# Layer 0's attention scores: the whole-array products of two tiles first, then the small products of both

## The chip, the cores and the metric

The kernel runs on one core of a Trainium2 chip. The core has five engines with queues of their own: TensorE (PE in the profile; PEld is its loading of weights), VectorE (DVE), ScalarE (ACT), GpSimd (POOL) and SyncE (SP), which here issues nearly all DMAs. Each engine works through its queue in order; engines wait for each other by semaphores. The metric is the device time of one execution in microseconds, less is better.

## What is computed

The reference is a decoder trunk of two layers over 256 tokens of width 1024, in float32. Layer 0 mixes tokens by dilated causal attention in three groups, layer 1 by gated linear attention; both are followed by a gated convolution FFN.

```python
A_CONFIGS = ((128, 1), (512, 4), (2048, 16))     # window, dilation
...
qkv = (h @ w_in).reshape(B, S, A_GROUPS, 3, A_HEADS, A_HEAD_DIM)
for g, (window, dilation) in enumerate(A_CONFIGS):
    o, lse = dilated_branch(q_g * scale, k_g, v_g, rel_bias_g, window, dilation)
...
wts = softmax(lses over the groups)
o = sum(wts * outs)
```

In a branch, token t attends to tokens t − j·dilation inside the window: s = q·k + bias, p = exp(s − max), o = p·v / sum. The softmax over the three groups' normalizers makes the whole one softmax over the keys of all three groups, which is how the kernel does it.

## The kernel before

**Split products.** Most weights are float32 and are multiplied in three passes: `split` loads 2048 columns into a raw buffer (L159, four buffers, shared with the chunks of `ada_chunk`, L133), ACT copies them to a rounded high part (L165, `whi`), DVE subtracts to get the low part (L168, `wlo`), and `mm3` multiplies high·high, low·high and high·low (L174 to L176).

**Units of layer 0.** The 16 heads are taken as eight units of two heads (`for u in range(NPAIR)`, L455). The weights of units 0 and 1 come with the first load. Each unit from 2 on projects q and k for three groups (tile `pqk`, three loads of 1 MB from `in_wqk`), and each from 1 on projects v (tile `pv`, two loads from `in_wv`). `evacuate` takes q and k out of PSUM: group 0's q becomes a high part on ACT (L434) and a low part on DVE (L435), one of each for each head; its k a high part on ACT (L439) and a low part on DVE (L440); groups 1 and 2 stay plain (L429, L430). `by_group` takes v out (L447 to L450). Between these, `next_ada` computes chunks of the conditioning products on DVE (L138).

**The attention of a unit** (`attend`, L356). The 256 tokens are in order of their residue modulo 4. There are four score tiles, one for each residue r, in PSUM banks of the tag `s`, of which there are three. A tile's rows are 64 queries of each of two heads. `shared` makes the columns of group 0: three products of the whole 128x128 array (L367), about 256 columns each. `dilated` adds 64 columns for group 1 and 64 for group 2: for each group and head one product of 64x64 (L374), which the profile records as two instructions. So a tile has four small products, eight records.

Tiles are handled in two pairs (h = 0, 1). DVE adds the bias and takes the maximum (L385, once a tile), negates it (L391, once a pair), ACT exponentiates (L394, once a tile), DVE takes the reciprocal (L395, once a pair) and scales the probabilities (L400 and L401, once a tile). PE transposes them (L405, three a tile), DVE and ACT in turn copy the result out (L406), and PE multiplies by v (L410, L414, tile `po`), which is again taken apart (L419 on ACT, L420 on DVE).

**What sets the order.** The program is written unit by unit, but the order on each engine is not the written one: a scheduler works on an estimated timeline when the program is built, and puts each instruction into its engine's queue. `behind(i)` adds one constraint, that what is made inside it is placed after instruction i in that order. In the built program the scores of a unit stand among the products of v and the next unit's projections. Once built, the order is fixed.

Of the kernel before, what the change touches and what calls it, by code (L numbers as in the profile page):

```python
# [57 lines left out]
def trunk(ctx: ExitStack, tc: tile.TileContext, I, out):  # L58
# [13 lines left out]
    def bank(name="ps", tag=None):  # L72
        tag = tag or next(cycle)
        return psum.tile([P, 512], F32, tag=tag, name=name, bufs={"p": 2, "s": 3, "t": 3}[tag])

    mm = nc.tensor.matmul
# [106 lines left out]
    def rstd_of(squares, n=D, tag=None):  # L183
        ps = bank("ms", tag)
        for i, sq in enumerate(squares):
            a = mm(ps[:, :T], ones_d, sq, start=(i == 0), stop=(i == len(squares) - 1))
        ln = tmp.tile([P, T], F32, tag="ln", name="ln", bufs=2)
        nc.scalar.activation(ln, ps[:, :T], AF.Ln, bias=eps[:, 0:1], scale=D / n)
        r = tmp.tile([P, T], F32, tag="rstd", name="rstd", bufs=2)
        norm_ops[:] = a, nc.scalar.activation(r, ln, AF.Exp, scale=-0.5)  # L190
        return r
# [29 lines left out]
    def by_residue(ap):  # L221

        return ap.rearrange("p (i r) -> p r i", r=4)

    def in_order(ap):

        return ap.rearrange("p (r i) -> p i r", r=4)

    def grouped(ap):
        return ap.rearrange("p (r i) -> p r i", r=4)  # L230

    def as_tokens(ap):
        return ap.rearrange("p (i r) -> p i r", r=4)
# [4 lines left out]
    @contextmanager  # L238
    def behind(*those):

        with ExitStack() as st:
            for i in those:
                st.enter_context(tc.issue_after(i.ins))
            yield
# [20 lines left out]
    def all_normed(l, sub):  # L265
        r = rstd_of([sums[0], sums[1], sums[2]])
        with behind(norm_ops[0]):
            keep_warm(6)
        return [normed(l, sub, r, kt) for kt in range(KT)]
# [45 lines left out]
    r = rstd_of([sq[:, 0, :], sq[:, 4, :]])  # L315
# [11 lines left out]
    w0, h = [], []  # L327
# [28 lines left out]
    def attend(u, q, k, v, bias):  # L356


        m = tmp.tile([P, 16], F32, tag="m", name="m")
        prob = [att.tile([P, KEYS + 3], F32, tag="prob", name="prob", bufs=6) for _ in range(4)]  # L360
        pt = att.tile([P, 4, KEYS], F32, tag="pt", name="pt")
        heads = [slice(E * hh, E * hh + E) for hh in range(2)]

        def shared(s, r):
            n = T + r + r % 2
            for i, (a, b) in enumerate(((0, 0), (1, 0), (0, 1))):
                mm(s[:, 0:n], q[0][a][:, r].rearrange("p a b -> p (a b)"), k[0][b][:, 0:n], start=(i == 0), stop=(i == 2))  # L367

        def dilated(s, r):
            own = slice(CH * r, CH * r + CH)  # L370
            for g in (1, 2):
                at = T + r + CH * (g - 1)
                for e in heads:
                    mm(s[e, at : at + CH], q[g][e, own], k[g][e, own], start=True, stop=True)  # L374

        for h in range(2):
            s = [bank("s", "s") for _ in range(2)]
            shared(s[0], 2 * h)
            dilated(s[0], 2 * h)
            shared(s[1], 2 * h + 1)  # L380
            dilated(s[1], 2 * h + 1)
            for i in range(2):
                r = 2 * h + i
                back = bass.AP(bias.tensor, bias.offset + KEYS - 1 + r, [bias.ap[0], [-1, KEYS + r]])
                nc.vector.tensor_tensor_reduce(  # L385
                    prob[r][:, 0 : KEYS + r], s[i][:, 0 : KEYS + r], back,
                    op0=ALU.add, op1=ALU.max, scale=1.0, scalar=-3e38, accum_out=m[:, r : r + 1],
                )
        for h in range(2):
            rs = slice(2 * h, 2 * h + 2)  # L390
            nc.vector.tensor_scalar(m[:, 4:8][:, rs], m[:, 0:4][:, rs], -1.0, None, op0=ALU.mult)  # L391
            for r in (2 * h, 2 * h + 1):
                c = prob[r][:, 0 : KEYS + r]
                nc.scalar.activation(c, c, AF.Exp, bias=m[:, 4 + r : 5 + r], accum_out=m[:, 8 + r : 9 + r])  # L394
            nc.vector.reciprocal(m[:, 12:16][:, rs], m[:, 8:12][:, rs])  # L395
            for r in (2 * h, 2 * h + 1):

                f = m[:, 12 + r : 13 + r]
                pn = att.tile([P, KEYS], F32, tag="pn", name="pn", bufs=3)
                nc.vector.tensor_scalar(grouped(pn[:, 0:T]), by_residue(prob[r][:, 0:T]), f, None, op0=ALU.mult)  # L400
                nc.vector.tensor_scalar(pn[:, T:KEYS], prob[r][:, T + r : KEYS + r], f, None, op0=ALU.mult)  # L401
                t = bank("t", "t")
                for j in range(3):
                    c = slice(P * j, P * j + P)
                    nc.tensor.transpose(t[:, c], pn[:, c], ident)  # L405
                (nc.vector.tensor_copy if r % 2 else nc.scalar.copy)(pt[:, r, :], t[:, 0:KEYS])  # L406
        po = bank("po", "t")
        for n in range(2):
            for hh, e in enumerate(heads):
                mm(grouped(po[e, :T]), v[n][:, e], pt[:, :, P * n + E * hh : P * n + E * hh + E], start=(n == 0), stop=False)  # L410
        for r in range(4):
            for hh, e in enumerate(heads):
                at = P * (r % 2) + P + E * hh
                mm(po[e, CH * r : CH * r + CH], v[r // 2][:, at : at + E],  # L414
                   pt[:, r, T + E * hh : T + E * hh + E], start=False, stop=(r == 3))
        hi = att.tile([P, T], F32R, tag=f"ohi{u}", name="ohi", bufs=1)
        lo = att.tile([P, T], F32R, tag=f"olo{u}", name="olo", bufs=1)
        src, hv, lv = in_order(po[:, :T]), as_tokens(hi), as_tokens(lo)
        nc.scalar.copy(hv, src)  # L419
        nc.vector.tensor_tensor(lv, src, hv.bitcast(F32), op=ALU.subtract)  # L420
        o_hi.append(hi)
        o_lo.append(lo)
# [32 lines left out]
    for u in range(NPAIR):  # L455
        with tc.issue_after(last_load[0].ins):
            bias = load_bias(u)
        q = [q_pair[u % 2]]
        k = [[att.tile([P, T + 4], F32R, tag=f"k0{i}", name="k") for i in range(2)]]
# [6 lines left out]
        if u == 0:  # L466
# [5 lines left out]
            for kt in range(KT):  # L472
                s, e = kt == 0, kt == KT - 1
# [11 lines left out]
        else:  # L485
            for g in range(NG):
# [3 lines left out]
                for kt in range(KT):  # L490
                    s, e = kt == 0, kt == KT - 1
# [15 lines left out]
        for n in range(2):  # L507
            by_group(v[n], pv[n], n)
        attend(u, q, k, v, bias)
        if u == 1:  # L510
            for n in range(2):
# [93 lines left out]
    h = all_normed(1, 0)  # L605
# [163 lines left out]
    for n in range(4):  # L769
        r = r_g[n // 2][:, 2 * (n % 2) : 2 * (n % 2) + 2, :]  # L770
        with behind(*norm_ops):
            silu = nc.scalar.activation(r, r, AF.Silu)
        for et in range(2):
            i = 2 * n + et
# [18 lines left out]
    def turned(tiles):  # L793
        for kt in tiles:
            for t, own in enumerate(halves):
                i = nc.tensor.transpose(y_ps[t][kt // 4][:, P * (kt % 4) : P * (kt % 4) + P], x[kt][:, own], ident)
        return i

    def mean_square(parts):
        for part in parts:  # L800
            for t, own in enumerate(halves):
                i = mm(ps[:, 2 * t : 2 * t + 2], sums[part][:, own], ones_d[:, 0:2], start=(part == t == 0), stop=(part == 2 and t == 1))
        return i

    with behind(last_pd[0]):
        last = mean_square(range(2))
    with behind(last):
        last = turned(range(2))
    with behind(last):
        last = mean_square([2])  # L810
# [4 lines left out]
    r = tmp.tile([P, 4], F32, tag="m", name="rstd")  # L815
# [111 lines left out]
```

## Time and profile before

| | us |
|---|---|
| median of 3 runs | 803.75 |
| lowest, highest | 802.86, 808.61 |
| the profiled execution | 802.44 |
| its span, first to last instruction | 800.7 |

The granted clock of TensorE is 0.995 of full speed over the span. The attention of layer 0 takes PE from 67 us (the first score product) to 285 us (the last product with v); the first FFN follows at 301 us. By tile, the whole-array score products are 96 instructions (L367) and the small ones 256 records (L374), the first at 66.7 and 67.4 us, the last at 273.2 and 273.6 us.

In the rows of a timeline, the first number is the start in us from the span's start, the second the length in us, then engine, line, operation, out<-in, shape and how many were merged; in square brackets stands how long the engine was idle before it and what ended that. Matmuls are pipelined and their ends are modelled, so the distance of two starts says more than a length. In the rows of waits the numbers are the total in us, how often, and the longest.

### The profile page before, as it was taken

To read this page: it belongs to the slowest core of one execution; us is meant where nothing else is said; L and a number is where in the kernel's file an instruction comes from. 1 tells how busy PE (TensorE), PEld (TensorE's weight loads), DVE (VectorE), ACT (ScalarE), POOL (GpSimd) and SP (SyncE) were. 2 spreads that over 40 slices of the span, in tenths; PEclk is the share of its full clock that TensorE was granted. 3 is DMA by queue.
4 is the path that set the end of the run, shared out by engine and by line. 5 is a ranking of instruction groups with operands and counts; after the bars stand their busy time and mean duration, and the time that the engine had idled before them with its cause. 6 is when DMAs were issued, how large, how long until landed. Compare 5 with 4: busy or idle time off the path is not lost.

```text
span 800.7 us, 15941 instructions
## 1 busy us (share of the span) xinstructions
PE 781.9 (98%) x6486; PEld 753.3 (94%) x6486; DVE 643.9 (80%) x1150; ACT 468.2 (58%) x869; POOL 15.2 (2%) x40
## 2 busy tenths in 40 slices
PE   7999999999999999999999999999999999999997
PEld 5999999999999989999999998889998999999997
DVE  6988978879778759999997877785468999988552
ACT  5556555555555546776765545744566866666442
POOL 1000000000000010000000100000010000000100
PEclk9899999999999999999999999999999999999999
DMA  8998577585685825886647793973343777644531
GB/s 343 418 334 298 202 280 278 202 329 197 248 312 200 301 85 204 301 301 223 240 162 249 268 332 127 366 261 108 106 156 109 275 269 248 251 141 159 181 110 53
DMA packets 32183, 184.72 MB, mean 231 GB/s; under 512 B 5804, under 2 KB 7340, under 8 KB 15470
## 3 DMA queue, kind: packets, MB, share of 16 engines
q1 hardware_dynamic: 32110, 183.70, 63.9%
q8 instruction: 51, 0.84, 0.4%
q14 instruction: 22, 0.18, 0.1%
HBM read 182.59 MB, written 1.10 MB: 229 GB/s over the span
## 4 chain that ended last, share of the span: by engine, by line
PE 89%; DVE 5%; DMA 3%; ACT 2%; issue 1%; SPq 0%; ACTq 0%; DVEq 0%
PE pab L176 10%; PE pab L175 10%; PE pab L174 10%; PE pqk L174 7%; PE pqk L175 6%; PE pqk L176 6%; PE pd L176 5%; PE pd L175 5%; PE pd L174 5%; PE pv L174 3%; PE pv L175 3%; PE pv L176 3%; DVE wlo L168 2%; PE py L175 2%; PE py L174 2%; PE s L367 2%
## 5 line engine op out<-in xcount | busy, mean ns | idle before, releaser
L168 DVE TENSOR_TENSOR wlo<-raw,whi 128x1024 fp32r<-128x1024 f32 (+2 forms) x274 | 295.8, 1107 | 55.6 <-ACT whi L165 54.8
L165 ACT CAST whi<-raw 128x1024 fp32r<-128x1024 f32 (+2 forms) x274 | 248.1, 954 | 152.4 <-PE pab L175 50.6
L174 PE MATMUL pab<-hhi,whi 128*128 128x256 f32 x704 | 194.0, 277 | 1.5 <-ACT hhi L252 1.5
L175 PE MATMUL pab<-hlo,whi 128*128 128x256 f32 x704 | 193.9, 276 | 0.5 <-DVE hlo L253 0.5
L176 PE MATMUL pab<-hhi,wlo 128*128 128x256 f32 x704 | 194.0, 276 | 0.4 <-DVE wlo L168 0.4
L174 PEld LDWEIGHTS pab<-hhi,whi 128*128 128x128 f32 x704 | 132.0, 188 | 2.2 <-ACT hhi L252 1.9
L175 PEld LDWEIGHTS pab<-hlo,whi 128*128 128x128 f32 x704 | 132.0, 188 | 0.9 <-DVE hlo L253 0.9
L176 PEld LDWEIGHTS pab<-hhi,wlo 128*128 128x128 f32 x704 | 132.0, 188 | 0.8 <-DVE wlo L168 0.8
L174 PE MATMUL pqk<-hhi,whi 128*128 128x256 f32 x448 | 123.5, 287 | 3.7 <-ACT hhi L252 3.2
L175 PE MATMUL pqk<-hlo,whi 128*128 128x256 f32 x448 | 125.0, 283 | 0.0
L176 PE MATMUL pqk<-hhi,wlo 128*128 128x256 f32 x448 | 124.9, 283 | 0.0
L138 DVE CUSTOM_DVE_ANT_0 ada_raw<-ada_raw,c_bc 128x1024 f32<-128x1024 f32 x96 | 113.5, 1218 | 4.5 <-DMA ada_raw<-in_w_ada 4.4
L176 PE MATMUL pd<-ghi,wlo 128*128 128x256 f32 x352 | 98.0, 280 | 0.6 <-DVE wlo L168 0.6
L175 PE MATMUL pd<-glo,whi 128*128 128x256 f32 x352 | 98.1, 280 | 0.0
L174 PE MATMUL pd<-ghi,whi 128*128 128x256 f32 x352 | 97.7, 279 | 0.0
L174 PEld LDWEIGHTS pqk<-hhi,whi 128*128 128x128 f32 x448 | 83.7, 191 | 5.5 <-ACT hhi L252 3.7
L175 PEld LDWEIGHTS pqk<-hlo,whi 128*128 128x128 f32 x448 | 85.0, 190 | 0.4
L176 PEld LDWEIGHTS pqk<-hhi,wlo 128*128 128x128 f32 x448 | 84.9, 190 | 0.2
L176 PEld LDWEIGHTS pd<-ghi,wlo 128*128 128x128 f32 x352 | 65.8, 187 | 0.8 <-DVE wlo L168 0.8
L175 PEld LDWEIGHTS pd<-glo,whi 128*128 128x128 f32 x352 | 66.0, 188 | 0.0
L174 PEld LDWEIGHTS pd<-ghi,whi 128*128 128x128 f32 x352 | 65.9, 188 | 0.0
L560 ACT ACTIVATE r<-pab,small 128x256 f32<-128x256 f32 x88 | 48.5, 559 | 11.7 <-DVE r L563 11.3
(184 smaller groups left out, 1248.2 us busy)
## 6 DMA issues: line engine op xcount, KB each, us to landing
ada_raw<-in_w_ada SPq DMA_DIRECT2D x47, 1024.0 KB, 6.7
raw<-in_w_up SPq DMA_DIRECT2D x44, 1024.0 KB, 5.2
raw<-in_w_down SPq DMA_DIRECT2D x32, 704.0 KB, 4.2
raw<-in_wqk SPq DMA_DIRECT2D x18, 1024.0 KB, 7.2
raw<-in_wv SPq DMA_DIRECT2D x14, 768.0 KB, 4.6
raw<-in_w SPq DMA_DIRECT2D x7, 960.0 KB, 6.6
raw<-in_w_out_a SPq DMA_DIRECT2D x4, 1024.0 KB, 6.9
raw<-in_w_v_b SPq DMA_DIRECT2D x4, 1024.0 KB, 6.7
```

Source lines behind the costliest of these rows:

```text
L138: nc.vector.tensor_tensor_reduce(w, w, c_bc, op0=ALU.mult, op1=ALU.add, scale=1.0, scalar=0.0, accum_out=dot,)
L165: copied[0] = nc.scalar.copy(hi[:, c], raw[:, c])
L168: last_lo[0] = nc.vector.tensor_tensor(lo[:, c], raw[:, c], hi[:, c].bitcast(F32), op=ALU.subtract)
L174: mm(ps, a[0], b[0], start=start, stop=False)
L175: mm(ps, a[0], b[1], start=False, stop=False)
L176: return mm(ps, a[1], b[0], start=False, stop=stop)
L367: mm(s[:, 0:n], q[0][a][:, r].rearrange("p a b -> p (a b)"), k[0][b][:, 0:n], start=(i == 0), stop=(i == 2))
L560: nc.scalar.activation(r, u[:, :T], AF.Identity, scale=cw[2], bias=col(C_CB + 44 * l + f))
```

## The change

```diff
         def shared(s, r):
             n = T + r + r % 2
             for i, (a, b) in enumerate(((0, 0), (1, 0), (0, 1))):
-                mm(s[:, 0:n], q[0][a][:, r].rearrange("p a b -> p (a b)"), k[0][b][:, 0:n], start=(i == 0), stop=(i == 2))
+                last = mm(s[:, 0:n], q[0][a][:, r].rearrange("p a b -> p (a b)"), k[0][b][:, 0:n], start=(i == 0), stop=(i == 2))
+            return last
...
         for h in range(2):
             s = [bank("s", "s") for _ in range(2)]
-            shared(s[0], 2 * h)
-            dilated(s[0], 2 * h)
-            shared(s[1], 2 * h + 1)
-            dilated(s[1], 2 * h + 1)
+            for i in range(2):
+                last_shared = shared(s[i], 2 * h + i)
+            with behind(last_shared):
+                for i in range(2):
+                    dilated(s[i], 2 * h + i)
```

The same products are made into the same banks. Of each pair of tiles, the whole-array products of both are written first, and the small products of both after them; `behind` holds all eight small products after the last whole-array product of the second tile.

## The prediction

> **What bounds the kernel now.** I read the page first, then the waits of each engine in the attention stage, then the order of time around the instructions that move.
>
> ```profile
> span 800.7 us, 15941 instructions
> PE 781.9 (98%) x6486; PEld 753.3 (94%) x6486; DVE 643.9 (80%) x1150; ACT 468.2 (58%) x869; POOL 15.2 (2%) x40
> PE 89%; DVE 5%; DMA 3%; ACT 2%; issue 1%; SPq 0%; ACTq 0%; DVEq 0%
> PE po L410 <- DVE pt L406: 0.7, 1, 0.7
> PE pqk L174 <- ACT v L450: 0.5, 1, 0.5
> PE py L174 <- ACT ohi L419: 0.5, 1, 0.5
> ```
>
> The first three lines are the page (busy time, and the chain that ended last); the last three are all that PE waits for from 55 to 290 us, in total, times and longest. So PE never stops in the attention but for 1.7 us: every nanosecond of PE time saved there should count. But that holds only while what PE consumes is ready earlier too. The waits of the other engines from 111 to 267 us (units 2 to 6) show a second round beside PE's:
>
> ```profile
> SPq L159 <- DVE dot L138: 30.3, 7, 5.8
> ACT whi L165 <- DMA raw<-in_wv: 27.6, 10, 4.2
> ACT whi L165 <- DMA raw<-in_wqk: 12.0, 8, 2.1
> ACT q L434 <- PE pqk L176: 1.5, 2, 0.9
> DVE wlo L168 <- ACT whi L165: 17.4, 10, 3.5
> DVE m L395 <- ACT prob L394: 6.9, 5, 1.4
> DVE q L435 <- ACT q L434: 0.9, 4, 0.4
> DVE k L440 <- ACT k L439: 0.6, 1, 0.6
> ```
>
> SP's loads wait for DVE to free a raw buffer, ACT waits for the load, DVE for ACT; these four DVE rows are all DVE waits in that window and none names PE. This is a round that paces itself. How far it runs ahead of PE is read at the transposes, from the end of DVE's scaled probabilities (L401) to the PE that reads them (L405), first row of tile in unit 2 and last in unit 6:
>
> ```profile
> 115.92 0.28 DVE L401 TENSOR_SCALAR pn<-prob,m 128x128 f32<-128x128 f32 x1
> 118.57 0.49 PE L405 MATMUL t<-ident,pn 128*128 128x128 f32 x3
> 249.71 0.28 DVE L401 TENSOR_SCALAR pn<-prob,m 128x128 f32<-128x128 f32 x1
> 250.14 0.49 PE L405 MATMUL t<-ident,pn 128*128 128x128 f32 x3
> ```
>
> The lead is 118.57 − 116.20 = 2.37 us in unit 2 and 250.14 − 249.99 = 0.15 us in unit 6. PE is the bound, but by the end of the attention only just.
>
> **The change, part by part.** First, what a visit to the small tiles costs. These are PE rows in order of time (start, length, instruction); starts are used, since ends are modelled:
>
> ```profile
> 115.35 0.52 PE L367 MATMUL s<-k,q 128*128 128x260 f32 x3
> 115.80 0.45 PE L374 MATMUL s<-k,q 64*64 64x64 f32 x8
> ...
> 142.47 0.45 PE L374 MATMUL s<-k,q 64*64 64x64 f32 x8
> 142.85 0.39 PE L174 MATMUL pqk<-hhi,whi 128*128 128x256 f32 x1
> 143.07 0.28 PE L175 MATMUL pqk<-hlo,whi 128*128 128x256 f32 x1
> 143.19 0.28 PE L176 MATMUL pqk<-hhi,wlo 128*128 128x256 f32 x1
> ...
> 268.94 0.56 PE L374 MATMUL s<-k,q 64*64 64x64 f32 x12
> 269.43 0.39 PE L174 MATMUL py<-ohi,whi 128*128 128x256 f32 x1
> ```
>
> A whole-array product comes every 0.12 us (143.07 to 143.19). Three of them ahead of a visit take 0.45, so 0.09 goes on the way in. Eight records of the small products (four of them, two records each) take 142.85 − 142.47 = 0.38; twelve take 0.49; so four more cost 0.11, and sixteen should take 0.60 where twice eight take 0.76: 0.16 saved. The first whole-array product after a visit takes 0.22 instead of 0.12: 0.10. One visit less with the same products is worth 0.09 + 0.16 + 0.10 = 0.35 us. Whether the small products themselves run faster in a longer visit no row shows; eight and twelve run at the same pace, so I take nothing for it.
>
> [...]
>
> The built programs of both kernels hold the same instructions; their orders are fixed when they are built. Before has 34 visits (some units are already joined or split by prefetched work), the changed one 18: 16 for the two pairs of eight units, and one more each in units 1 and 7, where the scheduler put transposes or products of v between. So PE is spared 16 × 0.35 = 5.6 us, some 0.7 a unit. SP's and POOL's orders are the same to the last instruction, and so is every engine's from the end of the attention on.
>
> Second, what the wait `behind(last_shared)` adds: the first tile's small products stand behind the second tile's shared ones, three more at 0.12, on PE only. Behind them in PE's queue are the next unit's projections, which do not depend on them. DVE's maximum of the first tile (L385) is later by under 0.5 us, and before it DVE stands in a load's wait anyway (L168 below). No cost.
>
> Third, and larger, what the scheduler does to DVE and ACT once the scores end at other times. These rows are one round, units 3 to 4, in order:
>
> ```profile
> 132.71 0.33 SPq L159 DMA_DIRECT2D raw<-in_wqk  x1
> 139.78 1.05 ACT L165 CAST whi<-raw 128x1024 fp32r<-128x1024 f32 x1 [2.06 <-DMA raw<-in_wqk]
> 140.86 1.23 DVE L168 TENSOR_TENSOR wlo<-raw,whi 128x1024 fp32r<-128x1024 f32 x1 [2.95 <-ACT whi L165]
> 147.12 0.17 DVE L395 RECIPROCAL m<-m 128x2 f32<-128x2 f32 x1 [1.38 <-ACT prob L394]
> 154.07 0.42 DVE L440 TENSOR_TENSOR k<-pqk,k 128x256 fp32r<-128x256 f32 x1
> 154.41 1.22 DVE L138 CUSTOM_DVE_ANT_0 ada_raw<-ada_raw,c_bc 128x1024 f32<-128x1024 f32 x1
> 162.69 1.83 DVE L168 TENSOR_TENSOR wlo<-raw,whi 128x768 fp32r<-128x768 f32 x2 [1.08 <-ACT whi L165]
> 164.55 0.33 SPq L159 DMA_DIRECT2D raw<-in_wqk  x1
> 186.77 0.42 DVE L440 TENSOR_TENSOR k<-pqk,k 128x256 fp32r<-128x256 f32 x1 [0.56 <-ACT k L439]
> ```
>
> The round takes 164.55 − 132.71 = 31.84 us. In the built order of the changed kernel the second L435 of a unit comes behind the four L400/L401 in units 2, 3, 5 and 6, where before both L435 stood ahead of them. L439 waits for it and L440 for L439. Unit 4 of before has this order already (last row): there L440 waits 0.56. So in these units L440, and the two L138 behind it that free the buffer for the next load of w_v, come later by that wait plus one L435, 0.43 us:
>
> ```profile
> 248.32 0.43 DVE L435 SCALAR_TENSOR_TENSOR q<-pqk,q 64x256 fp32r<-64x256 f32 x1
> ```
>
> which is 1.0 us a unit. Against it, the first pair's L391 no longer stands behind the third tile's L385, and in units 2, 4 and 6 the second pair's L391 no longer stands behind an L168 of 1.2 us.
>
> Put together at unit 6, the tightest place. The round enters it late by 1.0 each from units 2, 3 and 5, less what unit 4 gives back (its L440 keeps its time): between 0.7 and 1.5, and I take 1.2. The second pair's L391 is 1.2 earlier within the unit. So the last L401 ends where it did, and PE, whatever it saved before, stands there waiting. Between units 2 and 6 nothing is gained: 0, with ends of −2.0 (the round does not grow) and +2.0 (PE held by it longer). Units 0 and 1 lose theirs at 111 us, where PE already waits 0.5 for L450, which hangs on a load. Unit 7 goes from five visits to three with PE ahead of nothing but itself: 2 × 0.35 = −0.7.
>
> The sum: −0.7 us on the profiled execution of 802.44 us (span 800.7 and 1.7 around it), 801.7. The median of the runs, 803.75, lies 1.3 above that execution, so the forecast is 803.0.
>
> **Rivals.** *The whole saving arrives*: 5.6 us, 798.1. For it speaks that PE is 98% busy and that three of its waits are all there are; against it the lead of 0.15 us, which a fortieth of the saving uses up. [...]
>
> *The longer round wins (slower)*: the 1.0 us of units 2, 3, 5 and 6 adds up and unit 4 gives nothing back. PE is then carried by the round for five units: +4.0 − 0.7 = +3.3, 807.0. It decides as soon as the round's growth exceeds the lead plus the 1.2 us that L391 gains. For it: no DVE wait names PE, so nothing shortens the round when PE runs ahead. Against it: DVE still has idle time in front of L168 (2.95), though that idle is the load itself. A place where it would show early is the fourth tile's shared products, which need the bank of the first (three banks with the tag s): in unit 4 they stand behind 23 projections instead of 26, and both pairs come closer together:
>
> ```profile
> 171.77 0.39 PE L367 MATMUL s<-k,q 128*128 128x256 f32 x2
> ...
> 176.01 0.56 DVE L385 CUSTOM_DVE_ANT_0 prob<-s,bias 128x384 f32<-128x384 f32 x1
> ```
>
> The products of v end at 171.77; then come 0.09 + 0.60 for the visit, 0.22 for the first product after it and 23 × 0.12 = 2.76, so PE is there at 175.4, when DVE has read the first tile at 176.6. That is a PE wait of about 1.2 us in units 4 and 6, in place of the same wait at the transposes behind it, so it is no price of its own.
>
> *The change does not do what it says*: settled by the built order, but for the two split visits, which are in the count of 18.
>
> **How the numbers follow.** Forecast 0.58, whole saving 0.12, longer round 0.25, something unnamed 0.05. The likeliest is 803.0, with its own range 801.0 to 805.0 from the ends of the middle term. The range for eight in ten reaches to the longer round and its spread and leaves out most of the whole saving: 799.0 to 808.0. A measurement of this kernel tells a change from none at about 1%, 8 us. Faster than 795.7 would need more than the whole saving: 0.03. Slower than 811.8 would need twice the longer round, 8.0 − 0.7, or a wait of that size that I have not seen: 0.06. Within 1%: 0.91.
>
> **What would show it.** 18 visits, a visit of sixteen in 0.60 us: the price. Waits of PE in units 3 to 6 at L405 on L401 or at L367 on L385, some 0.5 to 1.5 us each, together 3 to 5 us: the forecast. No such waits and a shorter attention: the whole saving. L440 in units 3 and 5 later against its own unit's first L168 by about 1.0, and the w_qk loads further apart than 31.84: the longer round. The time would be wrong if the visit's price is not per visit, or if units 0 and 1, where DVE is nearly full, are reordered into a long wait.

## The result, and the profile after

| | before | after |
|---|---|---|
| median, us (20 runs each, on one chip) | 803.23 | 809.63 |
| lowest to highest | 801.10 to 808.61 | 802.53 to 819.72 |
| the profiled execution, its span | 802.44, 800.7 | 809.71, 807.7 |

The ratio of after to before is 1.0067, with a 95% interval of 1.0049 to 1.0086: the change made the kernel slower by about 5 us. Executions far above the fastest of their kernel are left out of the ratios and not read: two of after's 20 (814.62 and 819.72 us) and, among the experiments, the profiled ones of half_merged (863.57) and order_undone (2708.7). The forecast was 803.0 with a range of 799.0 to 808.0; the median lies above the range.

The page of after, in the lines that the prediction showed of before:

```profile
span 807.7 us, 15947 instructions
PE 782.0 (97%) x6486; PEld 756.4 (94%) x6486; DVE 643.8 (80%) x1150; ACT 467.8 (58%) x869; POOL 15.1 (2%) x40
PE 81%; DVE 10%; ACT 4%; DMA 4%; issue 2%; SPq 0%; ACTq 0%; DVEq 0%
```

PE's busy time is what it was (781.9), while the span is 7.0 us longer. The chain that ended last goes through PE for 81% where it was 89%; that share is no verdict by itself, as it is 72% and 82% in two executions of the fastest kernel below. What PE waited for from 55 to 290 us in after (total, times, longest):

```profile
PE pqk L174 <- ACT v L452: 5.5, 2, 2.9
PE pv L174 <- DVE k L432: 1.8, 1, 1.8
PE pqk L176 <- DVE wlo L168: 0.4, 1, 0.4
```

In before the first of these was 0.5 us, once, and the second did not show. To place the loss, I cut both executions at four PE rows: the first score product, the first product with v in units 2 and 7, the first product of the FFN. From the timeline of before:

```profile
66.75 0.40 PE L367 MATMUL s<-k,q 128*128 128x256 f32 x2
128.76 0.44 PE L410 MATMUL po<-pt,v 128*64 128x256 f32 x2
283.80 0.44 PE L410 MATMUL po<-pt,v 128*64 128x256 f32 x2 [0.74 <-DVE pt L406]
301.47 0.38 PE L174 MATMUL pab<-hhi,whi 128*128 128x256 f32 x1 [0.74 <-ACT hhi L252]
```

and of after:

```profile
64.69 0.52 PE L367 MATMUL s<-k,q 128*128 128x256 f32 x3
129.56 0.65 PE L412 MATMUL po<-pt,v 128*64 128x256 f32 x4
290.03 0.62 PE L412 MATMUL po<-pt,v 128*64 128x256 f32 x3 [0.50 <-DVE pt L408]
307.31 0.38 PE L174 MATMUL pab<-hhi,whi 128*128 128x256 f32 x1 [0.74 <-ACT hhi L252]
```

The differences, with the same cuts in an experiment of the next section beside them (v_first_again, whose rows start at 64.78, 124.15, 277.89 and 295.17):

| us | before | after | v_first_again |
|---|---|---|---|
| start to the first score | 66.75 | 64.69 | 64.78 |
| to unit 2's product with v | 62.01 | 64.87 | 59.37 |
| to unit 7's product with v | 155.04 | 160.47 | 153.74 |
| to the FFN | 17.67 | 17.28 | 17.28 |
| the rest of the span | 499.2 | 500.4 | 501.6 |

The attention (the middle three) is 234.72 us in before and 242.62 in after: 7.9 longer. The start, 2.1 earlier in after, differs among the executions read here by as much without any edit ahead of it (64.7 to 66.8).

How one of the two waits for v comes about is seen on ACT and PE in order of time. First PE in after:

```profile
106.32 0.68 PE L375 MATMUL s<-k,q 64*64 64x64 f32 x16
106.93 0.39 PE L367 MATMUL s<-k,q 128*128 128x258 f32 x1
110.24 0.58 PE L174 MATMUL pqk<-hhi,whi 128*128 128x256 f32 x1 [2.93 <-ACT v L452]
...
174.66 0.39 PE L367 MATMUL s<-k,q 128*128 128x258 f32 x1
177.67 0.58 PE L174 MATMUL pqk<-hhi,whi 128*128 128x256 f32 x1 [2.62 <-ACT v L452]
178.05 0.42 PE L175 MATMUL pqk<-hlo,whi 128*128 128x256 f32 x1
178.26 0.41 PE L176 MATMUL pqk<-hhi,wlo 128*128 128x256 f32 x1
```

and ACT in after:

```profile
107.01 1.99 ACT L165 CAST whi<-raw 128x1024 fp32r<-128x1024 f32 x2 [4.07 <-PE s L375]
108.90 0.36 ACT L449 COPY v<-pv 64x256 f32<-64x256 f32 x1
109.28 0.37 ACT L450 COPY v<-pv 64x256 f32<-64x256 f32 x1
109.66 0.26 ACT L451 COPY v<-pv 64x128 f32<-64x128 f32 x1
109.92 0.26 ACT L452 COPY v<-pv 64x128 f32<-64x128 f32 x1
```

The next unit's `pqk` takes a PSUM bank of the same tag as the two tiles `pv`, and that tag has two banks; one is free when ACT has copied the first tile of v out (L449 to L452, 1.3 us). In the built order these copies stand behind two L165 of the next unit's second w_qk load. That load was issued at 98.28 and landed at 106.91; the cast starts 0.10 us behind that, as 17 of the 23 casts of after that a load held up start 0.08 to 0.10 us behind a landing, so the load held ACT and not the PE product that the first row names. So v, which PE had finished before its small products at 106.32, waits for a load it has nothing to do with, then 2.0 us for the casts, and PE waits 2.93 us for the bank. Before has this order too at 108 us (there PE was ready 3.6 us later, at 110.87 against 107.31, and waited 0.5), but not at 168 us: there its copies came ahead of the casts. In after they stand behind them at both places. ACT at unit 4, first two rows of before, then two of after:

```profile
168.44 0.35 ACT L447 COPY v<-pv 64x256 f32<-64x256 f32 x1
171.65 2.00 ACT L165 CAST whi<-raw 128x1024 fp32r<-128x1024 f32 x2 [1.94 <-DMA raw<-in_wqk]
...
174.44 1.99 ACT L165 CAST whi<-raw 128x1024 fp32r<-128x1024 f32 x2 [3.74 <-DMA raw<-in_wqk]
176.33 0.36 ACT L449 COPY v<-pv 64x256 f32<-64x256 f32 x1
```

The second loss is in the last two PE rows: products that came every 0.12 us come every 0.21 (178.05 to 178.26). By stretches, the granted clock is the number ahead of the DMA share; after, and in the last row before:

```profile
100.00:107.00 7.00, 7.00 (x54) 6.68 (x52) 3.57 (x5) 2.47 (x4) 0.00 (x0) 1.00 1.01 407
107.00:110.00 3.00, 0.31 (x1) 0.11 (x1) 1.90 (x3) 2.96 (x6) 0.00 (x0) 0.83 0.75 317
110.00:114.00 4.00, 3.76 (x17) 3.76 (x18) 2.43 (x7) 2.18 (x8) 0.00 (x0) 0.50 0.30 74
114.00:118.00 4.00, 4.00 (x39) 3.80 (x38) 1.51 (x7) 1.94 (x3) 0.20 (x2) 0.77 0.48 201
...
177.20:180.60 3.40, 2.93 (x13) 2.93 (x14) 2.56 (x7) 1.69 (x7) 0.00 (x0) 0.51 0.23 94
...
110.00:114.00 4.00, 3.50 (x38) 3.12 (x37) 3.93 (x11) 1.79 (x7) 0.00 (x0) 1.00 0.76 256
```

After the wait TensorE runs at half clock: 17 products in 4 us, where the same 4 us of before hold 38 (some of them the short small products). The trace's records of the clock put the half clock at 108.98 to 115.81, 177.25 to 180.66 and 269.41 to 272.82 us, each time from within one of the three long waits on. In before the clock is 1.00 from 27.73 to 799.14 us, and so throughout the attention.

The parts add up to most of the 7.9 us, as an estimate from these rows: PE waits 8.7 us in after against 1.7 in before (55 to 295 us), 7.0 more; 11.9 us of work at half clock lose some 5.9; sixteen visits less, at the prediction's 0.35, give back 5.6. That makes 7.3.

### The profile page after: what moved, and what is told of

It reads as the page before. It is cut to its first block, busy times and chain, and to the rows that moved or that the text cites. A ratio compares the mean times of both kernels' runs of the same rounds, so it can differ in the third digit from the quotient of the medians.

```text
span 807.7 us, 15947 instructions
## 1 busy us (share of the span) xinstructions
PE 782.0 (97%) x6486; PEld 756.4 (94%) x6486; DVE 643.8 (80%) x1150; ACT 467.8 (58%) x869; POOL 15.1 (2%) x40
## 4 chain that ended last, share of the span: by engine, by line
PE 81%; DVE 10%; ACT 4%; DMA 4%; issue 2%; SPq 0%; ACTq 0%; DVEq 0%
PE pab L176 10%; PE pab L174 10%; PE pab L175 10%; PE pqk L176 5%; PE pqk L175 5%; PE pqk L174 5%; PE pd L175 5%; PE pd L176 5%; PE pd L174 5%; DVE wlo L168 4%; PE pv L174 3%; PE pv L175 3%; PE pv L176 3%; DMA raw<-in_wqk 2%; DVE ada_raw L138 2%
## 5 line engine op out<-in xcount | busy, mean ns | idle before, releaser
L168 DVE TENSOR_TENSOR wlo<-raw,whi 128x1024 fp32r<-128x1024 f32 (+2 forms) x274 | 295.7, 1109 | 59.0 <-ACT whi L165 56.1
L165 ACT CAST whi<-raw 128x1024 fp32r<-128x1024 f32 (+2 forms) x274 | 247.9, 954 | 151.6 <-PE pab L175 49.5
L175 PE MATMUL pqk<-hlo,whi 128*128 128x256 f32 x448 | 127.2, 288 | 0.5 <-DVE hlo L253 0.5
L138 DVE CUSTOM_DVE_ANT_0 ada_raw<-ada_raw,c_bc 128x1024 f32<-128x1024 f32 x96 | 113.6, 1219 | 2.7 <-DMA ada_raw<-in_w_ada 2.5
L174 PEld LDWEIGHTS pqk<-hhi,whi 128*128 128x128 f32 x448 | 85.5, 195 | 9.0 <-ACT v L452 5.9
L175 PEld LDWEIGHTS pqk<-hlo,whi 128*128 128x128 f32 x448 | 87.3, 195 | 1.0 <-DVE hlo L253 0.7
```

The lines of the kernel that those rows point to most:

```text
L138: nc.vector.tensor_tensor_reduce(w, w, c_bc, op0=ALU.mult, op1=ALU.add, scale=1.0, scalar=0.0, accum_out=dot,)
L165: copied[0] = nc.scalar.copy(hi[:, c], raw[:, c])
L168: last_lo[0] = nc.vector.tensor_tensor(lo[:, c], raw[:, c], hi[:, c].bitcast(F32), op=ALU.subtract)
L174: mm(ps, a[0], b[0], start=start, stop=False)
L175: mm(ps, a[0], b[1], start=False, stop=False)
```

## The experiments

In what follows the **casts** are the two L165 of a w_qk load, the **copies** the four L449 to L452 of v's first tile. The wait at 107 us is called unit 2's, that at 175 us unit 4's. The runs fell on three chips, so ratios to before on the same chip are compared: before took 803.05 us beside the first four experiments (v_first to keep_clock), 807.20 beside order_only, unit2_only, unit4_only and half_merged, and 804.28 beside order_undone and v_first_again. The waits of 3.1, 2.8, 2.0 and 0.56 us in the expectations are the 2.93, 2.62, 1.84 and 0.49 of the rows.

**v_first**, **v_first_before** and **vk_first**. The copies are put ahead of the casts, in after and in before, and for vk_first also k's last copy (L432) ahead of the subtraction that it waited behind in unit 7.

```diff
-        nc.scalar.copy(v[top, 2 * P : 3 * P], pv[low, P : 2 * P])
+        return nc.scalar.copy(v[top, 2 * P : 3 * P], pv[low, P : 2 * P])
...
-                w = split(I["wqk"][u - 2, g], 2048)
+                w = split(I["wqk"][u - 2, g], 2048, after=((v_out[0],),) * 2 if g in (1,) and u in (2, 3, 4, 5, 6, 7) else ((), ()))
...
-            by_group(v[n], pv[n], n)
+            v_out[n] = by_group(v[n], pv[n], n)
```

and for vk_first besides

```diff
-            last_lo[0] = nc.vector.tensor_tensor(lo[:, c], raw[:, c], hi[:, c].bitcast(F32), op=ALU.subtract)
+            with behind(*lo_after):
+                last_lo[0] = nc.vector.tensor_tensor(lo[:, c], raw[:, c], hi[:, c].bitcast(F32), op=ALU.subtract)
...
-            w = split(src[n], 2048)
+            w = split(src[n], 2048, lo_after=(k_out[0],) if (l, n) == (0, 0) else ())
```

> After, with one addition: ScalarE's two casts of a layer-0 weight load (L165, the group-1 load of units 2 to 7) are ordered behind its last copy of v's first tile of the unit before, so that the bank of pv never comes free behind a cast that waits for a load. 18 visits to the small tiles as after. Theory (v's copies behind the casts, and the half clock that follows each long wait): the waits of 3.1 us in unit 2 and 2.8 us in unit 4 on ScalarE's v copy go, and with them the half clock at 108.98 (6.83 us, worth 3.4) and at 177.25 (3.41 us, worth 1.7), 11 us in all at most: 799 to 803, and no granted clock of 0.5 between 100 and 190 us; unit 7's wait of 2.0 us on k stays. Rival (a round of ScalarE, VectorE and the loads that the reordering made longer): the waits turn up under other names, 807 to 810.

> Before, with the same addition, and so 34 visits: the control for the addition itself. Theory: only the 0.56 us wait in unit 2 can go, 802.5 to 803.5. Rival (the order of the casts is worth several us by itself, whatever the visits): 798 or less, or 806 or more.

> v_first, and VectorE's subtraction of the first in_w_out_a load (L168) ordered behind its last copy of k, for the wait of unit 7. Theory: the 2.0 us wait on k goes and the half clock at 269.4 (3.41 us, worth 1.7) with it, 2 to 3.7 us below v_first: 796 to 800. Rival (the end of the attention is set by the weight loads, not by PE): the same time as v_first.

Measured: v_first 797.71 us, ratio 0.9940 (0.9919 to 0.9961); v_first_before 804.81, 1.0028 (1.0008 to 1.0049); vk_first 798.37, 0.9941 (0.9920 to 0.9963). The waits for v are gone in v_first; the list of PE's waits from 55 to 295 us begins with

```profile
PE pv L174 <- DVE k L432: 1.0, 1, 1.0
PE po L412 <- DVE pt L408: 0.5, 1, 0.5
PE py L174 <- ACT ohi L421: 0.5, 1, 0.5
```

and no half clock shows in its attention. With one constraint after goes from 0.7% slower than before to 0.6% faster, a little below the bottom of the expected 799 to 803. The same constraint in before gains nothing: 804.81 lies 0.28% above before, between what its theory and its rival had, and why it is slower is open. The rival, a round made longer by the reordering, is refuted as the cause, since v_first keeps nearly all of after's order and is fast: SP's is the same, and in the attention ACT's differs in four casts alone, those of units 2 and 4, DVE's in eight instructions, six of them subtractions L168. (In layer 1, from 539 to 593 us, the scheduler moved some instructions as well. The span behind the attention is not shorter for it, 502.9 us against 500.4, and unit2_only and unit4_only below have no such change.) In vk_first the wait for k is gone as well (1.0 to nothing), the attention is 0.9 us shorter than in v_first by the same cuts (230.5 against 231.4), and the time is the same: a gain of this size is below what these runs separate, and the expected 2 to 3.7 us were not there, since the wait was already down to 1.0 and carried no half clock in v_first.

**keep_clock**. After, with dummy products behind unit 2's and unit 4's small products.

```diff
+            if h == 0 and u in (2, 4):
+                with behind(last_dilated):
+                    for i in range(6):
+                        mm(s[0][:, 400:496], ones_d, ones_d[:, :96], start=True, stop=True)
```

> After, and behind the small products of the first tile pair of units 2 and 4 six further products of 96 columns that write an unused part of a score bank (extra work, no part of the computation), so that TensorE stands still for about 1.8 and 1.5 us there in place of 2.9 and 2.8. The v copies stay where they are in after. Theory (half clock follows only a standstill longer than some 2 us): the waits end at the same time, the clock stays at 1 behind them, 5 us less than after: 804 to 806. Rival (the half clock costs nothing, because PE is not what the units wait for): 809 to 811.

Measured: 806.71, ratio 1.0054 (1.0035 to 1.0074), between the two expectations. The profiled execution (804.86 us) has the waits, shorter by the dummies, and yet the full clock; the PE wait, and the stretches around both:

```profile
PE pqk L174 <- ACT v L457: 3.3, 2, 2.4
```

```profile
105.00:115.00 10.00, 9.03 (x90) 8.32 (x89) 5.29 (x13) 5.92 (x14) 0.20 (x2) 1.00 0.76 298
172.00:182.00 10.00, 7.64 (x82) 6.92 (x81) 5.66 (x14) 6.28 (x14) 0.31 (x2) 1.00 0.75 289
```

Both waits end about when they did in after (110.34 and 176.97 against 110.24 and 177.67 us), so the dummies themselves gained PE little time; yet the attention took 237.8 us against 242.6. That speaks for a price of the half clock by itself. The 2 us of the theory were my estimate from the waits of the two profiles (1.84 us in after with half clock behind it, 0.49 in before without); unit 4's wait was still 2.4 us, not the 1.5 that was meant, and the clock stayed at 1.00 all the same (last section). The scheduler also moved other instructions here, so the 4.8 us need not be the clock's alone. In the other five executions the half clock may not be gone: their mean clock is 0.992 to 0.995 against 0.996 in this one, and they took 806.2 to 809.1 us. The runs of after point the same way without an edit: over the 18 executions that the ratio uses, the mean granted clock ranged from 0.986 to 0.996 and the time from 813.6 to 802.5, with a correlation of −0.74 and 6.8 us for each 0.01. Their mean clock was 0.9906 and before's, beside v_first, 0.9961 (24 runs), worth 0.0055 × 680 = 3.7 us, as an estimate at that slope.

**order_only** and **order_undone**. Is it the order that costs, or that TensorE comes earlier? A pair's products are joined in units 3 and 5 alone, so that PE saves almost nothing, while the built order still puts the copies behind the casts; order_undone has the constraint of v_first besides.

```diff
-            for i in range(2):
-                last_shared = shared(s[i], 2 * h + i)
-            with behind(last_shared):
+            if u in (3, 5):
                 for i in range(2):
+                    last_shared = shared(s[i], 2 * h + i)
+                with behind(last_shared):
+                    for i in range(2):
+                        dilated(s[i], 2 * h + i)
+            else:
+                for i in range(2):
+                    shared(s[i], 2 * h + i)
                     dilated(s[i], 2 * h + i)
```

> After, with two of a pair's products made together in units 3 and 5 alone, so 32 visits to the small tiles and not 18; ScalarE's order in units 2, 4 and 6 is nearly that of after, with v's copies behind the casts that wait for a load. Theory (a late copy costs only what TensorE comes early): TensorE comes to unit 4's first pqk as late as in before (174.4 us there, where casts and copies behind them would be done at 174.9 to 175.3), waits under 1 us and keeps its clock: 802 to 804.5. Rival (ScalarE's new order costs the whole by itself): 807 to 810.

> order_only (a pair's products together in units 3 and 5 alone; 31 visits here), with v's copies ahead of the casts in every unit. By ratio to before, because the chips differ. Theory (the place of v's copies is the whole of what order_only lost): its three waits for v (3.1 us in all) and the half clock behind one (1.7) go, 0.6% below order_only's 1.0063: 0.997 to 1.002. Rival (VectorE's order, which also changed, or the joined products themselves cost it): 1.004 to 1.008.

Measured: order_only 810.49, ratio 1.0063 (1.0037 to 1.0089); order_undone 803.37, 0.9975 (0.9949 to 1.0002). My expectation for order_only failed: the order, with next to none of the saving, costs as much as the whole change. Its waits and the granted clock behind unit 4's:

```profile
PE pqk L174 <- ACT v L457: 3.1, 3, 1.4
```

```profile
173.00:174.00 1.00, 0.00 (x0) 0.00 (x0) 0.95 (x4) 0.95 (x4) 0.00 (x0) 0.89 1.01 426
174.00:177.20 3.20, 3.16 (x15) 3.16 (x16) 2.64 (x8) 1.04 (x3) 0.00 (x0) 0.50 0.33 90
```

I had expected PE at unit 4's `pqk` at 174.4 us, as in before's profile; its last score product started at 172.4 here, because before's profiled execution had begun late. There are three such waits, 0.5 us in unit 2 as in before, 1.4 in unit 4 and 1.2 in unit 6, and a half clock of 3.4 us. In this execution the attention took 238.4 us, 3.7 more than in before; the 9.5 us that it lost behind the attention (508.7 us against 499.2) lie mostly in a slower pace of the products (last section). Against the theory as I had written it (a late copy costs only what TensorE comes early) stands its rival's number. That the copies' place is the whole of the loss is what order_undone shows, though a few instructions of VectorE moved there too; the next two runs are cleaner in this.

**unit2_only** and **unit4_only**: v_first's constraint for one of the two places, `u in (3,)` and `u in (5,)`, since the casts are of the next unit's load. Against after, two casts of ACT change places in unit2_only and four in unit4_only (two of them in unit 6), and three or four instructions of DVE.

> After, with v's copies put ahead of the casts in unit 2 alone. Theory (two waits, each with its half clock, and the second waits for what is gained before it): unit 2's wait goes; unit 4's grows from 2.8 us towards 4, because in v_first TensorE is ready for the bank at 169.7 us while the load lands at 170.2 and casts and copies end at 173.6. v_first and 4 us of waiting and 1.7 to 3.4 of half clock: 803 to 805. Rival (unit 2's wait is the cause, the rest follows from it): 798 to 799.5.

> After, with v's copies put ahead of the casts in unit 4 alone. Theory: unit 2's wait of 3.1 us stays, and with it a half clock of 3.41 or 6.83 us (worth 1.7 or 3.4); unit 4 keeps its clock and doesn't wait: v_first and 5 to 6.5, 802.5 to 804.5. Rival (what unit 4 loses is only hidden behind a load that is late anyway): 807 to 809.

Measured: unit2_only 1.0007 (0.9979 to 1.0035), unit4_only 1.0014 (0.9989 to 1.0040). On before's 803.05 of the first chip these are 803.6 and 804.2, as the theory had it: either place gives back about half. In unit2_only the wait of unit 4 was 2.8 us and not the 4 that I feared. In unit4_only the scheduler put the copies behind the casts in unit 6 instead, where PE then waited 2.4 us (the other 1.7 are unit 2's):

```profile
PE pqk L174 <- ACT v L452: 4.1, 2, 2.4
```

**half_merged**: v_first, the products joined in units 0 to 3 alone.

> v_first, with the products of a pair made together in units 0 to 3 alone: 27 visits, v's copies ahead of the casts throughout. Theory (each visit less is worth 0.36 to 0.44 us once nothing waits): between v_first (18 visits, 797.7) and the control with 34 (804.8), in proportion: 800.5 to 802. Rival (the gain comes from another part of the new order, not from the visits): at one of the two ends, 798 or 805.

**v_first_again**: v_first on another chip, beside order_undone.

> v_first once more, beside order_undone on the same chip, because its profiled execution was the slowest of its nine. Theory (14 visits less once nothing waits, 14 times 0.36 us = 5 us, less some waits for k and pt): 0.991 to 0.996 of before, and 0.4 to 0.8% below order_undone. Rival (v_first's gain was that of its chip): within 0.2% of order_undone.

Measured: half_merged 0.9958 (0.9936 to 0.9980) with 27 visits; v_first_again 798.01 us, 0.9922 (0.9892 to 0.9952) with 18. In order of visits, with the copies first: 34 at 1.0028, 31 at 0.9975, 27 at 0.9958, 18 at 0.9940 and 0.9922. The time falls with the visits, but not in proportion: the first step, three visits, is as large as the last thirteen, and from 31 on the intervals of neighbours overlap. half_merged was expected at 800.5 to 802 us beside before's 803.05, or 0.997 to 0.999, and came out a little lower. On one chip, order_undone to v_first_again is 13 visits and 0.53% of 804.28, 4.3 us: 0.33 us a visit. On another, v_first_before to v_first is 16 visits and 0.88% of 803.05, 7.1 us: 0.44. By the intervals of the ratios either is good to some 0.2, and the second holds what slowed v_first_before; against before itself v_first's two sets give 0.30 and 0.39. ACT and PE at unit 2 of v_first:

```profile
106.42 0.37 ACT L449 COPY v<-pv 64x256 f32<-64x256 f32 x1 [3.79 <-PE pv L176]
106.80 0.37 ACT L450 COPY v<-pv 64x256 f32<-64x256 f32 x1
107.18 0.26 ACT L451 COPY v<-pv 64x128 f32<-64x128 f32 x1
107.45 0.26 ACT L452 COPY v<-pv 64x128 f32<-64x128 f32 x1
107.61 2.00 ACT L165 CAST whi<-raw 128x1024 fp32r<-128x1024 f32 x2
```

```profile
106.84 0.68 PE L375 MATMUL s<-k,q 64*64 64x64 f32 x16
107.45 0.39 PE L367 MATMUL s<-k,q 128*128 128x258 f32 x1
107.76 0.38 PE L174 MATMUL pqk<-hhi,whi 128*128 128x256 f32 x1
```

The copies start when PE has made v and end at 107.71, and PE goes on into the bank at 107.76 without a wait. The casts begin at 107.61, 0.6 us later than in after, and no row of PE's waits names them. This version beats both kernels: 797.7 and 798.0 us in its two sets of runs.

## Why the prediction was wrong

**A visit's price: right.** Sixteen records were to take 0.60 us; from the first of them to the next product it is 106.93 − 106.32 = 0.61. There are 18 visits. The 0.35 us a visit came out as 0.33 and 0.44 between kernels with the copies first, with wide intervals. The saving of 5.6 us exists: v_first lies 0.6 to 0.8% below before, 4.8 to 6.3 us.

**`behind(last_shared)` costs nothing: nothing speaks against it.** It orders PE's own queue, so no wait could name it, and it was not tested by itself; but v_first, which has it too, gained about what the visits were to bring.

**The step that failed** is the third, "what the scheduler does to DVE and ACT once the scores end at other times". I followed L435, L440, L138 and L391 through the new order and put the middle of the attention at 0 with ends of ±2.0; it was +5.4 (160.47 − 155.04). The instructions that mattered are not among those: ACT's copies of v, which in unit 4 went behind the casts, so that a bank that PE needs hung on a load. That this order costs 0.6% with next to none of the saving is shown by order_only, that undoing it gives that back by order_undone, and that the saving then arrives by v_first. The delay of L440 that I did follow came as forecast (below), but it was not what PE waited for.

**"Units 0 and 1 lose theirs at 111 us, where PE already waits 0.5 for L450, which hangs on a load"**: I had the wait, and took for its price only what was saved before it, a sum of zero. The stretch grew by 2.9 (64.87 − 62.01), because the wait became 2.93 us and was followed by half clock. Against v_first_again it is 5.5 longer: some 3.3 more in gaps of over 0.6 us between two products, the other 2.2 in slower products.

**Unit 7, −0.7**: there PE waited 1.8 us for k at 267 us (L432, behind two L168), again with half clock behind it. Before has the same order on DVE without a wait: there the copy of k starts at 263.94 and PE goes on at 264.58. In after the copy starts 5.1 us later (269.02), as does the cast ahead of it that waits for a load, and PE is ready only 3.1 us later (267.65).

**The round.** The waits that were to show it, at L405 on L401 (L407 on L403 now), did not come. DVE ends the last scaled probabilities of unit 6 at 253.42 and PE reads them at 253.81:

```profile
253.15 0.27 DVE L403 TENSOR_SCALAR pn<-prob,m 128x128 f32<-128x128 f32 x1
253.81 0.49 PE L407 MATMUL t<-ident,pn 128*128 128x128 f32 x3
```

a lead of 0.39 us against 0.15 before, though PE had lost time on the way. In v_first_again, where PE waited for no v, the same lead is 0.96. But the middle stretch there is only 1.3 us shorter than in before (153.74), less than ten visits would bring (3.5 by the price), and PE's waits there are only 0.1 longer (0.83 against 0.74); how much of the rest the round takes, and how much the pace of the products (last section), stays open.

The two signs that the prediction named for the longer round did come in after. L440 (L442 now) starts 19.47 and 19.56 us behind its unit's first L168 of w_qk in units 3 and 5, where before has 18.52 and 18.14: 1.0 and 1.4 later. And three units' first w_qk loads, at 129.72 and 228.85 us, are 33.0 apart a unit, in before 31.9 (127.94 and 223.60). But in v_first_again L442 is as late (19.63 and 20.50), and the loads are 31.8 apart (124.38 and 219.66). So the later L442 does not stretch the round; with the waits for v gone, the round has its old length. As the cause of the loss it is out.

**The rival with the right number** was the longer round, 807.0, a chance of 0.25. Its mechanism, a later L440 that drives the w_qk loads apart by itself, is what v_first_again speaks against, so the closeness of its number is luck. What happened belongs to "something unnamed", to which I gave 0.05, and the last sentence on what would make it wrong ("reordered into a long wait") came nearest, though it looked at DVE. The change stayed within the 1% that the prediction gave its largest chance; the range ended 1.6 us too low.

## What to carry to other kernels

When a scheduler's order changes, list for each engine what stands ahead of the instructions that free a buffer which the bound engine needs, above all an instruction that waits for a load; the release counts, not only the work that was moved. Here a saving of an estimated 5.6 us on the bound engine turned into 7.0 us more of waiting at such places, with half clock worth an estimated 5.9 behind them; one constraint that put the release ahead of the load's consumer gave it back (from 0.7% slower than before to 0.6% faster).

## What the hardware showed that I had not expected

**The long waits cost nearly twice.** In after TensorE ran at half clock for 6.83, 3.41 and 3.41 us from within the waits of 2.93, 2.62 and 1.84 us on: the clock fell 1.67, 2.20 and 1.75 us after PE had stopped. To the 7.4 us of the three waits this adds the 5.9 estimated above. A wait of 1.85 us at 533.47 us, behind the attention, was followed by half clock too, from 535.65 to 539.06. In before the longest wait of PE from 65 to 785 us is 1.44 us, at 528.13, and the clock stays at 1.00. The length alone does not tell: 2.4 us in unit 4 of keep_clock and 2.4 us in unit 6 of unit4_only kept the clock at 1.00 (172 to 182 us and 220 to 260 us), and 1.38 us in unit 4 of order_only did not (0.50 from 174.0 to 177.2 us). The changes of the granted clock in after lie on a grid of 3.41 us: 108.98, 115.81, 177.25 and 269.41 are 2, 18 and 27 steps apart. What decides whether a wait is followed by half clock is open.

**The same products run at one of two paces.** In long stretches whole-array products of 256 columns come every 0.1133 us (before, 320 to 420 us), in others every 0.1178 (before, 740 to 790 us), at full granted clock. The same window in before and in order_only, 884 products against 851:

```profile
320.00:420.00 100.00, 100.00 (x884) 100.00 (x884) 96.86 (x174) 71.79 (x128) 0.00 (x0) 1.00 0.70 247
```

```profile
320.00:420.00 100.00, 100.00 (x851) 100.00 (x851) 93.23 (x164) 67.21 (x119) 0.00 (x0) 1.00 0.70 244
```

What takes 115 us at the faster pace takes 4.6 more at the slower, as an estimate from the two distances. From 620 to 700 us PE made 682 and 681 products in v_first and v_first_again, and 708 in before, which went over to the slower pace at 730. So stages are compared above and not only spans. That it makes the spread of some 5 us among a kernel's runs is likely and not shown, and what sets the pace is open.
